# A two-block network on one core: an early table load, a planner that knows more of its transfers, and new offsets

## The chip, the core and the metric

The kernel runs on one core of a Trainium2 chip. Time is device time of one execution in microseconds (us); lower is better. TensorE (PE) multiplies, VectorE (DVE), ScalarE (ACT) and GpSimd (POOL) work element by element, and transfers are issued from the queues of SyncE (SP) and ScalarE.

## The reference, cut to what matters

Sequence 256, width 1024, float32. `first_block` runs two layers, `second_block` two more:

```python
for i in range(2):                       # first_block
    x = x + 0.5 * swiglu(rmsnorm(x), gate, up, down)      # "ffn1", hidden 2816
    proj = rmsnorm(x) @ w_in                              # "mix1"
    x = x + concat(delta_rule_heads(proj), hyena(proj)) @ w_out
    x = x + 0.5 * swiglu(rmsnorm(x), gate, up, down)      # "ffn2"
x = rmsnorm(x)
for l in range(2):                       # second_block
    proj = rmsnorm(x) @ w_in_2                            # "mix2"
    x = x + (gated sum of attention, retention, short conv) @ w_out_2
    x = x + (silu(conv(h @ w_g)) * (h @ w_u)) @ w_ffn_out # "ffn3"
```

The mix1 part is a chunked delta rule (convolutions, a triangular solve) beside a Hyena branch, a long convolution in frequency space whose filter spectrum comes from a small network with three sines.

## The kernel before

All weights are cut on the host into 604 chunks of 128 x 1024 floats, in the order of use, and streamed through four buffers (`ws`). For each chunk ScalarE rounds to a high part (`wh`, in `split`) and another engine subtracts to get the low part (`wl`); TensorE then runs three products for each block (high by high, high by low, low by high) to keep float32 accuracy. The first two chunks (`HEAD`) are moved and split in halves (`pieces`). The operation tags `pmm` and `pacc` are the two kinds of PSUM buffer; `c` stands for working tiles, `sm` for small ones, `x` for the residual.

A generator (`drive`) notes the whole program as some thousands of operations with their dependences; nothing is sent to an engine yet. `Plan.place` then lists them on a modelled clock: every engine takes, of the operations that are ready and have buffers, the one of highest rank. A rank is the modelled length of work that still depends on the operation, plus an offset from the table `AHEAD`, looked up by stage and part (`"ffn1 norm0"` is the first norm in its stage, `" x0"`, `" cst"` and `" "` are parts of `setup`). The stage's letters are the first four of its name. An operation in `either` goes to GpSimd at every n-th of its kind, n from the table `POOL`, else to VectorE. `nc.hold` is the earliest modelled time. `emit` writes each engine's list in the planned order, so the order on each in-order queue is what the plan decides; the plan's times themselves are not sent.

What the plan assumes of transfers stands in few lines:

```python
if ops[i].dma and bus > t + BACK:        # too much is under way: try later
...
hw = max(hw, t) + o.dma
now[e] = t + .06 if e != "POOL" else t + 1.1
bus = max(bus, hw + .8) + o.cost         # cost: bytes / 360e3 us
o.end = bus
```

`setup` issues x in four pieces of two feature tiles each (with the first gain) on ScalarE's queue, then the constants `cst` and the parameters `par`; `prep` makes high and low parts of x times gain and the squares, `norm` the token sums, their inverse root (`rsqrt_m`, eleven small VectorE operations) and `spread`, two transposes that turn it into the tile `r`. `spectra` (three sines, five results of each order written to DRAM as `ds`) runs as a side task, and `hyena` reads `ds` back; both use ScalarE's queue for it. The delta rule's `dn_solve` sends blocks through DRAM (`dg`, `dv`) on SyncE's queue.

Of the kernel before, what the change touches and what calls it, by code (L numbers as in the profile page):

```python
# [14 lines left out]
AF = mybir.ActivationFunctionType  # L15
# [9 lines left out]
EPS = 1e-6  # L25
CW = 1024
A3 = (2,)
BACK = 5
AHEAD = {' cst': -57, ' prep': 0, ' sq0': 25, ' x0': 82, 'conv': 5, 'cst': -50, 'da': 40, 'decay': 10, 'double': -20, 'ffn1 finish': 60, 'ffn1 norm': 110, 'ffn1 norm0': 5, 'ffn1 prep': 10, 'ffn1 sq': 25, 'ffn2 finish': -4, 'ffn2 prep': 40, 'ffn2 scaled': 0, 'ffn2 spec': 85, 'ffn2 split': 5, 'ffn3 finish': -40, 'ffn3 norm': 0, 'ffn3 prep': 40, 'ffn3 scaled': 42, 'ffn3 split': -7, 'ffn3 sq': 48, 'finish': 82, 'g0': 5, 'hyena': 10, 'kk': -10, 'mix1 double': 30, 'mix1 finish': 83, 'mix1 hyena': 20, 'mix1 kk': 10, 'mix1 out': 78, 'mix1 prep': 38, 'mix1 qk': 66, 'mix1 solve': 20, 'mix1 sq': 32, 'mix1 w': 3, 'mix2 finish': 12, 'mix2 norm': 162, 'mix2 prep': -40, 'mix2 ret': 95, 'mix2 split': -22, 'mix2 sq': 5, 'norm': 153, 'norm0': 152, 'out': 80, 'prep': 10, 'qk': 23, 'ret': 168, 'solve': 10, 'spec': 80, 'split': -2, 'sq': 28, 'sq0': 40, 'w': 8, 'x0': 2}
WIN = 1500  # L30
LOCK = True
RG = 2
SLACK = 2
HEAD = 2
NARROW = 5
PAD = 0.05
POOL = {'ba': 1, 'by': 1, 'gate': 4, 'hg': 3, 'ht': 2, 'hx0': 2, 'hx1': 4, 'hx3': 2, 'mask': 1, 'rot': 4, 'rvg': 1, 'sc': 2, 'sc1': 6, 'se': 4, 'v1': 6, 'wo2': 2}
GATES = [("gate", 0), ("gate", 1), ("gate", 2)] + [(k, m + 3 * (k == "gate")) for m in range(5) for k in ("br", "gate")] + [("br", m) for m in (5, 6, 7)]
WS, WP = 4, 4
HALF = (1, 0)  # L40
# [283 lines left out]
class Plan:  # L324
# [43 lines left out]
    @staticmethod  # L368
    def cost(eng, call, out, ins, kw):
        n = int(np.prod(out.shape[1:]))  # L370
        in_psum = any(a.tensor.space == PSUM for a in ins if type(a.tensor).__name__ == "Tile")
        if call == "dma_start":
            return out.shape[0] * n * 4 / 360e3 * (1.0 if n > 300 else 1.6)
        if eng == "PE":
            if call != "matmul":
                return .109
            n = int(np.prod(ins[-1].shape[1:]))
            if ins[-1].dtype == F32R:
                return .0049 + max(n, 256) * .0004426
            return 2 * (.005 + max(2 * n, 256) * .000418)  # L380
        n = max([n] + [int(np.prod(a.shape[1:])) for a in ins])
        ptr = sum(1 for a in ins[1:] if int(np.prod(a.shape[1:])) == 1 and n > 1)
        if eng == "DVE":
            if call == "memset":
                return .01 + n / 970
            one = call in ("tensor_scalar", "tensor_copy") and not in_psum
            return .068 + n * (.00052 if one else .00104) + .061 * ptr
        if eng == "ACT":
            return (.052 if in_psum else .094) + n * .000833 + .093 * (ptr + ("accum_out" in kw))
        if eng == "POOL":  # L390
            if call == "memset":
                return .035 + n / 1200
            return .15 + n * {"tensor_tensor": .0021, "affine_select": .00087}.get(call, .0031)
        raise AssertionError((eng, call))
# [46 lines left out]

    def lag(self, a, b):
        if a.dma:
            return .95
        return self.LAG.get((a.eng, b.eng), .25 if b.eng == "PE" else .13)

    def place(self):
        ops = self.ops
# [53 lines left out]
        pend = {e: [] for e in now}  # L502
        events = [0.0]
        back, far, lo = [], [], 0
        hw = bus = 0.0
        port = {"DVE": 0.0, "POOL": 0.0}
        table = None
        done = 0
# [5 lines left out]
        while done < len(ops):  # L514
# [10 lines left out]
            for e in now:  # L525
                while pend[e] and pend[e][0][0] <= t + 1e-9:
                    i = heapq.heappop(pend[e])[1]
                    heapq.heappush(wait[e], (-ops[i].rank, i))
                if now[e] > t + 1e-9:
                    continue  # L530
                skip, got = [], None
                while wait[e]:
                    r, i = heapq.heappop(wait[e])
                    if i > lo + WIN:
                        heapq.heappush(far, (i, r))
                        continue
                    if LOCK and ops[i].port and port[e] > t + 1e-9:
                        skip.append((r, i))
                        heapq.heappush(events, port[e])
                        continue  # L540
                    if ops[i].dma and bus > t + BACK:
                        skip.append((r, i))
                        heapq.heappush(events, bus - BACK)
                        continue
                    need = {}
                    for nm in ops[i].tiles:
                        if nm not in held:
                            need[self.tag[nm]] = need.get(self.tag[nm], 0) + 1
                    short = [g for g, n in need.items() if free[g] < n]
                    if short:  # L550
                        parked[short[0]].append((e, r, i))
                    elif i > lo and not safe(i):
                        unsafe.append((e, r, i))
                    else:
                        got = i
                        break
                for s in skip:
                    heapq.heappush(wait[e], s)
                if got is None:
                    continue  # L560
                o = ops[got]
                for nm in o.tiles:
                    if nm not in held:
                        held[nm] = True
                        free[self.tag[nm]] -= 1
                        live[self.tag[nm]][lo:span[nm][0]] += 1
                o.start = t
                if got == lo:
                    while lo < len(ops) and ops[lo].start is not None:
                        lo += 1  # L570
                    wake(unsafe)
                    heapq.heappush(events, t)
                while far and far[0][0] <= lo + WIN:
                    i, r = heapq.heappop(far)
                    heapq.heappush(wait[ops[i].eng], (r, i))
                    heapq.heappush(events, t)
                if o.dma:
                    hw = max(hw, t) + o.dma
                    now[e] = t + .06 if e != "POOL" else t + 1.1
                    bus = max(bus, hw + .8) + o.cost  # L580
                    o.end = bus
                else:
                    c = o.cost
                    if o.flex and e == "POOL":
                        c = o.flex
                    if o.table is not None and o.eng == "ACT":
                        s = "sin" if o.table == AF.Sin else "exp" if o.table in (AF.Exp, AF.Tanh) else table
                        if s != table:
                            c += 1.3
                            table = s  # L590
                    if e == "PE":
                        c += 1.7 * min(max(t - now[e] - 1.1, 0.0) / 2.2, 1.0)
                    now[e] = o.end = t + c
                    if o.port:
                        port["POOL" if e == "DVE" else "DVE"] = o.end
                heapq.heappush(events, now[e])
                done += 1
                for j in o.succs:
                    p = ops[j]
                    p.left -= 1  # L600
                    p.ready = max(p.ready, o.end + self.lag(o, p))
                    if not p.left:
                        heapq.heappush(pend[p.eng], (max(p.ready, t), j))
                        heapq.heappush(events, max(p.ready, t))
                for nm in o.tiles:
                    todo[nm] -= 1
                    last[nm] = max(last[nm], o.end)
                    if not todo[nm]:
                        live[self.tag[nm]][lo:span[nm][1] + 1] -= 1
                        x = last[nm] + (1.0 if o.dma else .2)  # L610
                        heapq.heappush(back, (x, self.tag[nm]))
                        heapq.heappush(events, x)
# [12 lines left out]
class Build:  # L625
# [316 lines left out]
    def setup(self):  # L942
# [13 lines left out]
            nc.scalar.dma_start(out=xg[:, c], in_=A["x"][:, c])  # L956
        nc.part = "cst"
        nc.scalar.dma_start(out=self.cst, in_=A["cf"])
        nc.part = ""
        nc.scalar.dma_start(out=self.par, in_=A["par"])  # L960
        nc.hold = 12.0
        self.rounded(self.cr.rearrange("p a b -> p (a b)"), A["cr"])
# [1148 lines left out]
```

## Time and profile before

| | us |
|---|---|
| median of 3 runs | 1942.88 |
| lowest and highest | 1941.55, 1950.27 |
| profiled execution, its own time | 1946.58 |
| span of the profiled execution | 1944.9 |

The span runs from the first to the last instruction of the program in the profiled execution; 1.7 us of that execution's time lie around it. All of the helpers' operations carry one line number, so the profile is read by tile names.

### The profile page before, as it was taken

Reading aid. Unit: us, or ns where it says so; the run is one execution under the profiler, and the core shown is the slowest. Engines: PE = TensorE matmul, PEld = TensorE weight load, DVE = VectorE, ACT = ScalarE, POOL = GpSimd, SP = SyncE. Lnnn points to the kernel's source line nnn. Section 1 sums busy time; section 2 is a strip of 40 time slices with the busy share of each in tenths; the row PEclk is TensorE's granted clock in tenths of the full one; section 3 lists DMA queues with packets and bytes.
Section 4 is the critical chain, followed back from the end, with each engine's and each line's share of the span. In section 5 each row is a group of like instructions: output and inputs, shape, how many; then the busy total and the mean of one; then the engine's idle time right before and its main releaser. Section 6 shows DMA issues by size and latency. Waiting matters only on the chain.

```text
span 1944.9 us, 36536 instructions
## 1 busy us (share of the span) xinstructions
PE 1910.2 (98%) x14038; PEld 1800.6 (93%) x14038; DVE 1509.2 (78%) x3067; ACT 1090.5 (56%) x1792; POOL 213.1 (11%) x218
## 2 busy tenths in 40 slices
PE   7999998999999999999999999999999999999999
PEld 7998997999999999998999999999999999999998
DVE  7768879986669667899886679766977788669776
ACT  5656664565556555664555565455655654556564
POOL 0000041000000000222000002233000012240000
PEclk9999998999999999999999999999999999999999
DMA  8655763255555556552565544555555544555553
GB/s 293 212 185 170 230 195 103 91 197 189 184 186 178 189 186 217 201 149 85 166 195 186 189 167 163 180 185 187 183 186 192 174 153 161 191 182 191 188 185 130
DMA packets 127046, 348.84 MB, mean 179 GB/s; under 512 B 24758, under 2 KB 39960, under 8 KB 126872
## 3 DMA queue, kind: packets, MB, share of 16 engines
q1 hardware_dynamic: 115584, 326.89, 51.3%
q10 hardware_dynamic: 11288, 19.63, 2.9%
q8 instruction: 110, 1.80, 0.4%
q14 instruction: 64, 0.52, 0.1%
HBM read 333.61 MB, written 11.81 MB: 178 GB/s over the span
## 4 chain that ended last, share of the span: by engine, by line
PE 91%; DVE 5%; ACT 1%; DMA 1%; issue 1%; ACTq 0%; POOL 0%; SPq 0%; DVEq 0%; POOLq 0%
PE pmm L621 57%; PE pacc L621 35%; DVE c L621 4%; DVE wl L621 1%; ACT c L621 1%; ACTq L621 0%; ACT wh L621 0%; DVE sm L621 0%; DVE x L621 0%; DMA ds<-c 0%; DMA c<-dv 0%; DMA ws<-in_W 0%; DMA x<-in_x 0%; POOL c L621 0%; ACT L621 0%
## 5 line engine op out<-in xcount | busy, mean ns | idle before, releaser
L621 PE MATMUL pmm<-c,wh 128*128 128x256 f32 (+1 forms) x4576 | 1102.4, 322 | 9.9 <-ACT wh L621 8.6
L621 ACT ACTIVATE wh<-ws 128x1024 fp32r<-128x1024 f32 (+1 forms) x604 | 635.6, 1055 | 537.0 <-PE pmm L621 221.3
L621 DVE TENSOR_TENSOR wl<-ws,wh 128x1024 fp32r<-128x1024 f32 (+1 forms) x562 | 687.7, 1226 | 270.9 <-ACT wh L621 265.0
L621 PE MATMUL pmm<-c,wl 128*128 128x256 f32 x3056 | 859.6, 281 | 0.1
L621 PEld LDWEIGHTS pmm<-c,wh 128*128 128x128 f32 x4576 | 759.8, 189 | 81.1 <-ACT wh L621 8.6
L621 PEld LDWEIGHTS pmm<-c,wl 128*128 128x128 f32 x3056 | 577.6, 189 | 1.0 <-DVE wl L621 0.6
L621 PE MATMUL pacc<-c,wh 128*128 128x256 f32 x3136 | 566.9, 281 | 0.0
L621 PEld LDWEIGHTS pacc<-c,wh 128*128 128x128 f32 x3136 | 482.6, 189 | 6.1 <-issue 0.7
L621 PE MATMUL pacc<-c,wl 128*128 128x256 f32 x1568 | 440.5, 281 | 0.0
L621 PEld LDWEIGHTS pacc<-c,wl 128*128 128x128 f32 x1568 | 296.0, 189 | 0.0
L621 ACT ACTIVATE c<-c 128x256 fp32r<-128x256 f32 (+4 forms) x412 | 181.2, 450 | 157.2 <-DVE c L621 144.3
L621 DVE TENSOR_TENSOR c<-c,c 128x256 f32<-128x256 f32 (+7 forms) x345 | 166.9, 497 | 7.9 <-ACT c L621 4.4
L621 DVE TENSOR_TENSOR c<-pmm,c 128x256 f32<-128x256 f32 (+1 forms) x292 | 134.5, 461 | 41.9 <-PE pmm L621 36.0
L621 DVE SCALAR_TENSOR_TENSOR c<-c,c 128x256 f32<-128x256 f32 (+3 forms) x288 | 129.3, 450 | 14.3 <-ACT c L621 7.7
L621 POOL TENSOR_TENSOR wl<-ws,wh 128x1024 fp32r<-128x1024 f32 x42 | 104.2, 2480 | 263.3 <-ACT wh L621 145.0
L621 DVE SCALAR_TENSOR_TENSOR c<-c,par,c 128x256 f32<-128x256 f32 x248 | 114.7, 482 | 22.9 <-ACT c L621 21.7
L621 PE MATMUL pacc<-c,c 128*128 128x128 f32 (+5 forms) x700 | 98.9, 302 | 2.8 <-DVE c L621 1.4
L621 ACT ACTIVATE c<-pacc 128x512 f32<-128x512 f32 (+4 forms) x125 | 59.2, 495 | 64.3 <-PE pacc L621 60.2
L621 POOL TENSOR_TENSOR c<-c,c 128x256 f32<-128x256 f32 (+1 forms) x50 | 60.9, 1222 | 291.6 <-DVE c L621 245.5
L621 PEld LDWEIGHTS pacc<-c,c 128*128 128x128 f32 (+2 forms) x700 | 83.1, 195 | 8.9 <-DVE c L621 2.3
L621 ACT ACTIVATE c<-c,par 128x256 f32<-128x256 f32 x96 | 52.8, 574 | 51.0 <-DVE c L621 50.4
L621 DVE TENSOR_TENSOR c<-pacc,c 128x512 f32<-128x512 f32 (+4 forms) x126 | 72.0, 610 | 9.3 <-PE pacc L621 6.6
(85 smaller groups left out, 997.6 us busy)
## 6 DMA issues: line engine op xcount, KB each, us to landing
ws<-in_W SPq DMA_DIRECT2D x600, 512.0 KB, 3.4
ds<-c ACTq DMA_DIRECT2D x20, 256.0 KB, 4.7
c<-ds ACTq DMA_DIRECT2D x20, 256.0 KB, 3.8
c<-dv SPq DMA_DIRECT2D x32, 128.0 KB, 2.7
dv<-c SPq DMA_DIRECT2D x8, 256.0 KB, 5.0
dg<-c SPq DMA_DIRECT2D x8, 256.0 KB, 3.2
c<-in_cm ACTq DMA_DIRECT2D x6, 256.0 KB, 5.0
ws<-in_W SPq DMA_DIRECT2D x4, 256.0 KB, 6.4
```

The costliest lines, as they stand in the source:

```text
L621: getattr(e, call)(*a, **kw)
```

## The change

ScalarE gets one Tanh of four zeros early in `setup`, on a tile that VectorE clears; nothing reads its result. The planner's transfers are costed at 330e3 bytes per us for 360e3; the bus is taken as busy up to 3.0 at the start; a transfer may not be planned while the eighth before it is unfinished (`lanes`); an issue takes .35 on ScalarE's queue for .06 (GpSimd's 1.1 goes too, but no transfer is issued there); a transfer on ScalarE's queue that depends on another is planned 6.5 behind its end for .95; the allowed backlog `BACK` is 3.0 for 5. The whole table `AHEAD` and the table `POOL` have new values.

```diff
-BACK = 5
-AHEAD = {' cst': -57, ' prep': 0, ' sq0': 25, ' x0': 82, 'conv': 5, ..., 'ffn1 norm0': 5, ..., 'hyena': 10, 'mix1 hyena': 20, 'mix1 qk': 66, 'mix1 solve': 20, 'norm': 153, ...}
+BACK = 3.0
+AHEAD = {' ': 65.0, ' cst': 43.0, ' prep': -38.0, ' sq0': 177.0, ' table': 111.0, ' x0': 68.0, 'conv': -109.0, ..., 'ffn1 norm0': 428.0, ..., 'hyena': -12.0, 'mix1 hyena': 32.0, 'mix1 qk': 400.0, 'mix1 solve': 83.0, 'norm': 302.0, ...}
-SLACK = 2
+SLACK = 2.0
-POOL = {'ba': 1, 'by': 1, 'gate': 4, 'hg': 3, 'ht': 2, 'hx0': 2, 'hx1': 4, 'hx3': 2, 'mask': 1, 'rot': 4, 'rvg': 1, 'sc': 2, 'sc1': 6, 'se': 4, 'v1': 6, 'wo2': 2}
+POOL = {'br': 3, 'hg': 6, 'ht': 2, 'hx0': 2, 'hx1': 3, 'mask': 1, 'rot': 4, 'rvg': 1, 'sc': 2, 'sc1': 3, 'se': 4, 'sh': 4, 'sq': 6, 'wo2': 4}
...
-            return out.shape[0] * n * 4 / 360e3 * (1.0 if n > 300 else 1.6)
+            return out.shape[0] * n * 4 / 330e3 * (1.0 if n > 300 else 1.6)
...
         if a.dma:
-            return .95
+            return 6.5 if b.dma and b.eng == "ACT" else .95
...
-        hw = bus = 0.0
+        hw, bus = 0.0, 3.0
+        lanes = [0.0] * 8
...
-                    if ops[i].dma and bus > t + BACK:
+                    if ops[i].dma and max(bus - BACK, lanes[-8]) > t:
                         skip.append((r, i))
-                        heapq.heappush(events, bus - BACK)
+                        heapq.heappush(events, max(bus - BACK, lanes[-8]))
...
-                    now[e] = t + .06 if e != "POOL" else t + 1.1
+                    now[e] = t + (.06 if e == "SP" else .35)
                     bus = max(bus, hw + .8) + o.cost
                     o.end = bus
+                    lanes.append(bus + .2)
...
         nc.scalar.dma_start(out=self.cst, in_=A["cf"])
-        nc.part = ""
+        nc.part, nc.hold = "table", .35
+        z = self.T("sm", [128, 2, 2])
+        nc.vector.memset(z[:, 0], 0.0)
+        self.act(z[:, 1], z[:, 0], AF.Tanh)
+        nc.part, nc.hold = "", 0.0
         nc.scalar.dma_start(out=self.par, in_=A["par"])
```

## Rows read from the trace of the kernel before

**Rows 1.** The page, busy time of each engine, its share of the span, instructions.

```profile
PE 1910.2 (98%) x14038; PEld 1800.6 (93%) x14038; DVE 1509.2 (78%) x3067; ACT 1090.5 (56%) x1792; POOL 213.1 (11%) x218
```

**Rows 2.** Waits of PE, whole span: us in total, times, longest us.

```profile
PE pacc L621 <- DVE c L621: 8.6, 13, 1.2
PE pmm L621 <- ACT wh L621: 8.6, 1, 8.6
...
PE pacc L621 <- DVE sm L621: 3.5, 2, 3.0
```

**Rows 3.** The chain that ended last, first 60 us: start us, us, what.

```profile
0.80 4.10 DMA x<-in_x
...
4.92 0.33 ACTq L621
...
5.28 1.28 ACT L621
...
6.58 1.43 ACT c L621 x3
...
13.93 4.38 DMA ws<-in_W
...
18.33 0.33 ACTq L621
...
18.70 0.44 ACTq L621
```

**Rows 4.** The groups by line, ACT's table loads: count, busy us, mean ns, idle before.

```profile
L621 ACT ACT_TABLE_LOAD x13 | 16.7, 1283 | 5.5 <-DMA x<-in_x 5.3
```

**Rows 5.** Timeline of DVE, 6 to 26 us: start us, us, what, idle before and its end.

```profile
16.75 0.15 DVE L621 TENSOR_SCALAR sm<-pacc 128x2 f32<-128x2 f32 x1
20.29 1.23 DVE L621 TENSOR_TENSOR wl<-ws,wh 128x1024 fp32r<-128x1024 f32 x1 [3.38 <-ACT wh L621]
```

**Rows 6.** Windows of the start: us, busy by engine (PE, PEld, DVE, ACT, POOL), PEclk, DMA, GB/s.

```profile
8.58:21.10 12.52, 12.42 (x76) 11.67 (x76) 9.11 (x17) 7.57 (x15) 0.00 (x0) 1.00 0.90 327
21.10:24.10 3.00, 0.00 (x1) 0.00 (x1) 2.69 (x14) 2.13 (x3) 0.00 (x0) 1.00 1.03 395
...
25.00:29.00 4.00, 4.00 (x24) 4.00 (x23) 3.38 (x10) 2.83 (x7) 1.01 (x1) 0.57 0.92 287
```

**Rows 7.** Timeline of ACT, 240 to 262 us, its queue and engine.

```profile
253.27 0.48 ACTq L621 DMA_DIRECT2D c<-in_hyf  x1
...
253.78 1.54 ACTq L621 DMA_DIRECT2D c<-in_cdec  x2
255.36 0.75 ACTq L621 DMA_DIRECT2D c<-in_hyf  x1
256.16 1.06 ACT L621 ACTIVATE wh<-ws 128x1024 fp32r<-128x1024 f32 x1 [2.26 <-PE pacc L621]
```

**Rows 8.** Windows around mix1 of either layer, and mix2: columns as Rows 6.

```profile
200.00:262.00 62.00, 59.16 (x427) 54.86 (x426) 48.36 (x118) 36.98 (x62) 13.71 (x17) 0.97 0.71 232
...
300.00:330.00 30.00, 22.68 (x133) 19.20 (x131) 26.60 (x60) 12.73 (x27) 6.69 (x7) 0.83 0.42 114
...
780.00:835.00 55.00, 54.05 (x431) 52.02 (x431) 47.93 (x126) 35.41 (x56) 8.90 (x14) 1.00 0.62 211
835.00:925.00 90.00, 83.68 (x650) 79.40 (x649) 87.18 (x224) 50.57 (x100) 20.27 (x20) 0.96 0.39 108
...
1270.00:1400.00 130.00, 130.00 (x1093) 129.74 (x1092) 93.81 (x153) 71.63 (x107) 35.08 (x30) 1.00 0.57 185
...
1350.00:1400.00 50.00, 50.00 (x418) 49.74 (x417) 46.66 (x93) 30.32 (x49) 0.92 (x7) 1.00 0.61 199
```

**Rows 9.** Groups by shape, DVE and POOL: count, busy us, mean ns, idle before.

```profile
L621 DVE TENSOR_TENSOR wl<-ws,wh 128x1024 fp32r<-128x1024 f32 x558 | 685.1, 1230 | 270.9 <-ACT wh L621 265.0 <-PE pmm L621 2.5
...
L621 DVE TENSOR_TENSOR c<-c,c 128x256 f32<-128x256 f32 x138 | 58.4, 423 | 3.2
...
L621 POOL TENSOR_TENSOR c<-c,c 128x256 f32<-128x256 f32 x32 | 34.2, 1075 | 59.7 <-DVE c L621 58.8
```

More of the change, by code (lines that the diff above doesn't have):

```diff
@@ L27 @@
 A3 = (2,)
-BACK = 5
-AHEAD = {' cst': -57, ' prep': 0, ' sq0': 25, ' x0': 82, 'conv': 5, 'cst': -50, 'da': 40, 'decay': 10, 'double': -20, 'ffn1 finish': 60, 'ffn1 norm': 110, 'ffn1 norm0': 5, 'ffn1 prep': 10, 'ffn1 sq': 25, 'ffn2 finish': -4, 'ffn2 prep': 40, 'ffn2 scaled': 0, 'ffn2 spec': 85, 'ffn2 split': 5, 'ffn3 finish': -40, 'ffn3 norm': 0, 'ffn3 prep': 40, 'ffn3 scaled': 42, 'ffn3 split': -7, 'ffn3 sq': 48, 'finish': 82, 'g0': 5, 'hyena': 10, 'kk': -10, 'mix1 double': 30, 'mix1 finish': 83, 'mix1 hyena': 20, 'mix1 kk': 10, 'mix1 out': 78, 'mix1 prep': 38, 'mix1 qk': 66, 'mix1 solve': 20, 'mix1 sq': 32, 'mix1 w': 3, 'mix2 finish': 12, 'mix2 norm': 162, 'mix2 prep': -40, 'mix2 ret': 95, 'mix2 split': -22, 'mix2 sq': 5, 'norm': 153, 'norm0': 152, 'out': 80, 'prep': 10, 'qk': 23, 'ret': 168, 'solve': 10, 'spec': 80, 'split': -2, 'sq': 28, 'sq0': 40, 'w': 8, 'x0': 2}
+BACK = 3.0
+AHEAD = {' ': 65.0, ' cst': 43.0, ' prep': -38.0, ' sq0': 177.0, ' table': 111.0, ' x0': 68.0, 'conv': -109.0, 'cst': -119.0, 'da': -84.0, 'decay': -170.0, 'double': 63.0, 'ffn1 finish': 51.0, 'ffn1 norm': 525.0, 'ffn1 norm0': 428.0, 'ffn1 prep': 22.0, 'ffn1 scaled': -1.0, 'ffn1 spec': 80.0, 'ffn1 split': -2.0, 'ffn1 sq': 210.0, 'ffn2 ': 5.0, 'ffn2 finish': 206.0, 'ffn2 norm': 257.0, 'ffn2 prep': 477.0, 'ffn2 scaled': -39.0, 'ffn2 spec': 71.0, 'ffn2 split': 92.0, 'ffn2 sq': 211.0, 'ffn3 ': 0.0, 'ffn3 finish': -79.0, 'ffn3 norm': 51.0, 'ffn3 prep': 126.0, 'ffn3 scaled': 129.0, 'ffn3 split': -69.0, 'ffn3 sq': -140.0, 'finish': 188.0, 'hyena': -12.0, 'kk': 139.0, 'mix1 ': -1.0, 'mix1 conv': 5.0, 'mix1 decay': 10.0, 'mix1 double': 267.0, 'mix1 finish': -134.0, 'mix1 hyena': 32.0, 'mix1 kk': 10.0, 'mix1 norm': 249.0, 'mix1 out': 87.0, 'mix1 prep': 81.0, 'mix1 qk': 400.0, 'mix1 solve': 83.0, 'mix1 split': -2.0, 'mix1 sq': 13.0, 'mix1 w': 3.0, 'mix2 da': 40.0, 'mix2 finish': 10.0, 'mix2 norm': 157.0, 'mix2 prep': -127.0, 'mix2 ret': 167.0, 'mix2 split': -157.0, 'mix2 sq': -113.0, 'norm': 302.0, 'norm0': -78.0, 'out': 72.0, 'prep': -329.0, 'qk': 234.0, 'ret': 123.0, 'scaled': -344.0, 'solve': 55.0, 'spec': -6.0, 'split': -74.0, 'sq': -34.0, 'sq0': -38.0, 'table': 17.0, 'w': 20.0, 'x0': 190.0}
 WIN = 1500
```

## The prediction

> **What bounds the kernel now.** I read the busy times first, then PE's waits, then the chain and the windows of the stretches in which PE stood. PE is busy 1910.2 of 1944.9 us [rows 1], and the change takes no product away, so what it can give back is PE's idle time, 34.7 us, and what a lower TensorE clock costs just after an idle stretch. Of the waits, one of 8.6 us is the start, before the first product, and one of 3.0 us comes a little later, on a small DVE tile; the waits on DVE's working tiles are 13, 8.6 us together [rows 2]. The windows show where these lie: around mix1 of both layers, with DVE near its limit. PE is full in the window of mix2 that I took [rows 8].
>
> **The start, step by step.** The chain shows the first piece of x in flight from 0.80 for 4.10 us, an issue on ACT's queue at 4.92, the table load of 1.28 us at 5.28, three operations on x, and only then the first split of weights [rows 3]. The 13 loads of the run are one here and two around each of six sines, at 1283 ns each [rows 4], so one load serves all functions but the sine. The Tanh takes the load ahead of x's landing if it stands in ACT's queue before the issue that waits at 4.92 (it starts 0.02 us after x landed: a transfer waits for an earlier one to finish, which is what the new limit of eight models). In the new plan the backlog limit of 3.0 holds up further issues as soon as the first pieces are under way, ACT then has nothing else ready, and the Tanh goes in behind the first piece of x. I take the whole 1.3 us. Below, the gain is nothing if the waiting issue still stands ahead, and the price is up to 1.6 us if the other three pieces of x, now issued behind memset, load and Tanh, become what is late (the load's 1.28 and about 0.3 for the two small operations, an estimate from the small DVE row of 0.15 [rows 5]). What would hide the load is the 4.10 us of x.
>
> Here the Trainium skill has another price: "ScalarE: Activation LUTs", section "What ACT_TABLE_LOAD costs", adds a drain of about 1380 ns to a load's 1283. The trace shows the 1283 but no drain: the next operation starts at 6.58, 1.30 behind the load's start [rows 3]. By the page the head would give 2.7 us and the sum below would be 1.4 lower.
>
> Next the norm. DVE does its first small operation at 16.75, then stands 3.38 us in front of a split at 20.29 whose high part is not made [rows 5], with the rest of the inverse root behind it; PE stands from 21.10 to 24.10, and at 25 to 29 its granted clock is 0.57 of full, most of that time at the lower level, which costs 0.43 x 4.00 = 1.7 us [rows 6]. The high part was late because ACT's queue stood: its issue at 18.33 starts 0.02 us behind the landing of a weight chunk (13.93 + 4.38), then one more issue of 0.44 [rows 3]. Both causes are addressed: the offset of this norm goes from 5 to 428, far ahead of the splits, and the limit of eight puts blocking issues elsewhere. Without the split in front, the inverse root ends before PE needs it. So 3.0 + 1.7 are open, with the load 6.0. But the chunk split at 20.29 is ready at 21.5 and PE, 1.3 us ahead, would want it at 19.8: 1.7 us late next, if its landing does not move. I give back 1.5: **-4.5** for the start. Bounds: -6.0 and +1.6.
>
> Against more speak the transfers: their engines are busy 0.90 and 1.03 of the time from 8.58 to 24.10 [rows 6]. If that is the limit the chunk cannot land earlier, and the start gives only the 2.6 us from 21.5 to 24.1. The Trainium skill, "DMA: Bandwidth & Descriptors", section "Issuing engines are not separate DMA queues", says why it may be: transfers of all queues share the same engines and interleave, so another order of issue moves bytes, it does not add any.
>
> **Layer 0 before mix1's end.** From 200 to 262, PE is idle 2.84 us and the clock of 0.97 costs some 1.8 [rows 8]. Four issues fill ACT's queue from 253.27 to 256.11, 0.69 us each, and a split waits behind them [rows 7]; the old plan gave them 0.06, the new one 0.35. What is late after them is that split's chunk. I take the longest of the waits here, near 1.1, and half of the clock: **-2.0**. Bounds 0 and -4.6. The 6.5 behind a dependent transfer acts on the same queue, for `ds`; it is in this term.
>
> **The ends of mix1.** From 300 to 330, PE is idle 7.32 us, and the clock of 0.83 costs 0.17 x 22.68 = 3.9; from 835 to 925, 6.32 and 0.04 x 83.68 = 3.3 [rows 8]. Together 20.8, the largest sum that the offsets can reach. But DVE is busy 26.60 of 30 and 87.18 of 90 there: the stall ends only if DVE work is done before or behind these stretches. There is room before: 13.6 us free from 200 to 262, 7.1 from 780 to 835. Chains bind, though: the delta rule cannot start before its projections. And the new POOL table gives DVE splits in mix1: the two of `ba`, two of `hx3`, one of `v1`, less one of `hx1`, net four at 1.23 [rows 9], 4.9 us, where DVE is the limit. Between +4.9 and -14 (two thirds), I take a third: **-7.0**, nearer to the full DVE than to its free room ahead.
>
> **Other edits.** In mix2 each layer's DVE gets six `gate` splits (7.4), sixteen `by` additions at 0.42 (6.8) and two `wo2` splits (2.5) and gives three `br` splits (3.7): 13.0 net [rows 9]. DVE's free time hides them, 36.2 of 130 us [rows 8]; without that cover they cost what the third rival says. The bandwidth of 330 and the bus at 3.0 move only orders and are in the start. A new order makes new waits: I add three at the mean of 0.66 us (8.6 over 13) [rows 2], **+2.0**; below nothing is not to be had from this.
>
> **Sum.** -4.5 - 2.0 - 7.0 + 2.0 = -11.5. The profiled execution took 1946.58, span 1944.9 and 1.7 around it: 1935.1. It stands 3.7 above the median of the three runs, 1942.88, so the median should come to 1931.4.
>
> **Rivals.**
> First: the ends of mix1 stay, because DVE has no room that its chains can use. Speaking for it, 87.18 of 90; against it, the free room ahead. Then -4.5 - 2.0 + 2.0: 1938.4; with the 4.9 us of returned splits, 1943.3.
> Second: the load does not get ahead, being queued behind the issue that waits for x. For it, the two waits of 0.02 us behind a landing; against it, the backlog limit. The forecast loses 1.3: 1932.7. It may go with any case and decides none. The full transfer engines at the start are of this kind too: 4.5 becomes 2.6, 1933.3.
> Third, on the other side: DVE becomes the bound at mix2's end. In the last 50 us of that stage DVE is busy 46.66, 3.3 free [rows 8]; POOL's additions take 1075 ns and DVE's 423 [rows 9], but POOL's ran beside it. Once more than 3.3 of the 13.0 us fall into that stretch, PE waits; with all of them it is 9.7 a layer, 19.4 for both. On the first rival's time this is 1957.8. Against it: most gates come earlier, where DVE has its room.
> Fourth: all of the start, 6.0, all of layer 0's lead, 4.6, and two thirds of the ends, 14, less the 2.0: 1942.88 - 22.6 = 1920.3.
>
> **How the numbers follow.** Forecast 0.55, with 1925 to 1937 as its own range; first rival 0.22; third 0.10; fourth 0.10; 0.03 for some slower mishap without a name. 0.5% is 9.7 us, about what the runs can tell from no change: faster means under 1933.2, slower over 1952.6. The forecast's own range puts two thirds below that line, 0.37; with the fourth, faster 0.47. The rest of the forecast, 0.18, and the first rival make 0.40 for the same; slower 0.13. From 1919 to 1946 the range leaves out the third rival and the nameless one, 0.13, and about half of the fourth.
>
> **What would show it.** The load starting near 1.3 to 3 us and the first product near 7.3; no wait of PE of 3 us on a small DVE tile; the clock not falling near 25; ACT's queue without a row of issues in front of a split near 253; PE's idle time around mix1's ends down from 13.6 to some 9. The forecast is wrong if DVE in those windows is as full and PE as idle as now, or if new PE waits on `wl` stand at the end of mix2.

## The result, and the profile after

The changed kernel takes 1925.03 us, the median of four runs (1923.67 to 1925.60); the kernel before, in the same comparison, 1945.37 (1941.55 to 1950.27). The ratio is 0.9893, with an interval of 0.9867 to 0.9919: 1.1% faster, clear of the scatter. Beside the experiments the kernel before has medians of 1942.87, 1944.94 and 1943.91, so the gain is 18 to 21 us. The profiled execution's span is 1923.8 us for 1944.9, 21.1 less. The execution profiled before took 1946.58, 1.2 to 3.7 us above the medians of its kernel, so not all of the 21.1 is the change's.

The page of the changed kernel, the first line busy time by engine (us, share of the span, instructions); then PE's waits (us in total, times, longest us):

```profile
PE 1900.1 (99%) x14038; PEld 1794.1 (93%) x14038; DVE 1533.7 (80%) x3106; ACT 1087.9 (57%) x1791; POOL 157.0 (8%) x180
```

```profile
PE pmm L623 <- ACT wh L623: 7.4, 2, 6.6
PE pacc L623 <- DVE c L623: 5.3, 8, 2.4
PE pacc L623 <- ACT c L623: 2.7, 4, 1.4
PE pmm L623 <- DVE wl L623: 2.2, 2, 1.1
PE pacc L623 <- POOL c L623: 1.5, 1, 1.5
```

PE's idle time is 1923.8 - 1900.1 = 23.7 us, for 34.7 [rows 1]. The wait of 3.0 us on a small DVE tile [rows 2] is gone, and the waits on DVE's working tiles are 8 with 5.3 us, for 13 with 8.6. DVE gained 24.5 us of work and lies at 80%, POOL lost 56: work went from the engine that had time to the much fuller one, and PE stands less all the same. A fuller DVE did not cost PE time here.

To see where the 21.1 us came from, both spans are cut where the same amount of PE's work is done (after product 500, 2000, 5500 and 9500 of the 12336 products of a working tile `c` with a weight's `wh` or `wl`; the PE counts of the pairs agree within two). First the kernel before, then the changed one; columns as in [rows 6].

```profile
0.00:83.70 83.70, 72.02 (x508) 68.12 (x509) 62.60 (x120) 48.54 (x79) 3.91 (x12) 0.98 0.78 262
83.70:386.60 302.90, 292.64 (x2075) 270.47 (x2073) 247.83 (x572) 173.50 (x293) 43.45 (x47) 0.98 0.51 163
386.60:955.90 569.30, 561.75 (x4076) 527.28 (x4075) 450.20 (x913) 318.64 (x528) 38.87 (x45) 0.99 0.55 178
955.90:1533.70 577.80, 576.83 (x4283) 546.69 (x4282) 436.91 (x835) 323.48 (x527) 65.16 (x64) 1.00 0.55 182
1533.70:1944.90 411.20, 406.92 (x3106) 387.99 (x3104) 311.71 (x630) 226.36 (x368) 61.69 (x50) 1.00 0.52 172
```

```profile
0.00:79.60 79.60, 71.09 (x507) 67.61 (x508) 60.73 (x113) 45.99 (x77) 5.32 (x13) 0.98 0.81 276
79.60:375.30 295.70, 289.82 (x2077) 268.42 (x2075) 250.28 (x580) 173.44 (x293) 38.63 (x44) 0.99 0.51 169
375.30:937.70 562.40, 557.53 (x4076) 525.18 (x4075) 450.00 (x913) 318.30 (x529) 39.72 (x47) 0.99 0.54 179
937.70:1512.00 574.30, 574.00 (x4282) 544.07 (x4281) 448.04 (x854) 323.48 (x527) 37.93 (x45) 1.00 0.54 183
1512.00:1923.80 411.80, 407.63 (x3106) 388.83 (x3104) 324.63 (x649) 226.66 (x368) 35.46 (x31) 1.00 0.51 172
```

| stretch, by work | length | of it, PE's idle time |
|---|---|---|
| the start | -4.1 | -3.2 |
| to the end of layer 0's mix1 | -7.2 | -4.4 |
| to the end of layer 1's mix1 | -6.9 | -2.7 |
| layer 0 of the second block and beyond | -3.5 | -0.7 |
| the rest | +0.6 | -0.1 |
| together | -21.1 | -11.0 |

(Length is the difference of the first numbers of two lines; idle time is the first less the second number.) So the gain lies where the prediction looked, the start and both mix1 parts, but 3.5 us come from a stretch where none was expected, and nearly half of the whole is not idle time.

The start of the changed kernel, ACT's timeline (start us, us, queue or engine, what, how many, idle before and its end):

```profile
0.80 0.42 ACTq L623 DMA_DIRECT2D x<-in_x  x1
1.25 1.28 ACT L623 ACT_TABLE_LOAD   x1 [1.25 <-PEq L2106]
1.31 1.35 ACTq L623 DMA_DIRECT2D x<-in_x  x3
2.54 0.20 ACT L623 ACTIVATE sm<-sm 128x2 f32<-128x2 f32 x1
4.99 1.03 ACT L623 ACTIVATE c<-x 128x512 f32<-128x512 f32 x2 [2.24 <-DMA x<-in_x]
...
10.79 0.33 ACTq L623 DMA_DIRECT2D cst<-in_cf  x1
```

The load runs at 1.25, beside the three other issues of x, and the first operation on x starts at 4.99 for 6.58 [rows 3]. The issue of `cst`, which stood at 4.92 just behind x's landing [rows 3], is now at 10.79. What PE meets then:

```profile
6.59 0.80 PE L623 MATMUL pmm<-c,wh 128*128 128x256 f32 x2 [6.59 <-ACT wh L623]
...
13.21 0.50 PE L623 MATMUL pmm<-c,wh 128*128 128x256 f32 x2 [0.84 <-ACT wh L623]
```

The first product comes 2.0 us sooner than the 8.6 of [rows 2], but 0.84 us is lost again at 12.37, where the next chunk's high part is late.

The windows of the changed kernel that answer to [rows 6, 8]:

```profile
12.37:14.79 2.42, 0.50 (x3) 0.30 (x2) 2.10 (x4) 2.42 (x5) 0.50 (x1) 1.00 0.71 224
15.00:19.00 4.00, 4.00 (x22) 4.00 (x22) 3.01 (x6) 0.95 (x1) 0.00 (x0) 0.57 0.86 286
200.00:262.00 62.00, 62.00 (x480) 59.19 (x480) 55.54 (x140) 39.27 (x65) 12.59 (x14) 1.00 0.67 231
290.00:330.00 40.00, 34.16 (x237) 30.54 (x236) 36.45 (x85) 20.02 (x41) 10.18 (x11) 0.91 0.33 91
780.00:835.00 55.00, 55.00 (x450) 53.78 (x449) 49.66 (x134) 36.79 (x66) 16.47 (x19) 1.00 0.71 227
835.00:925.00 90.00, 85.13 (x645) 80.23 (x644) 88.09 (x258) 45.46 (x81) 12.65 (x13) 0.96 0.36 112
```

The lead of layer 0's mix1 (200 to 262) has no idle time left and a full clock. Of the 1.9 us that PE stands from 12.37 to 14.79, 0.84 and 1.08 are waits for a weight's high and low part; the granted clock then falls (0.57 from 15 to 19, as it was from 25 to 29). At the ends of mix1 PE still stands 5.84 and 4.87 us, for 7.32 and 6.32, and DVE is as full as before.

How much of the clock is the change's? In the run e17 (below) TensorE's 14038 products stand in the very order of the kernel before. Here is one window of the kernel before, then two of e17:

```profile
220.00:223.00 3.00, 3.00 (x16) 3.00 (x15) 3.00 (x13) 0.63 (x1) 0.00 (x0) 0.50 0.52 177
```

```profile
200.00:262.00 62.00, 60.38 (x451) 56.31 (x450) 49.79 (x123) 37.95 (x63) 15.48 (x17) 1.00 0.70 231
220.00:223.00 3.00, 3.00 (x24) 2.87 (x24) 3.00 (x11) 1.73 (x3) 0.00 (x0) 1.00 0.22 76
```

In the kernel before the clock stood at its lower level from 220 to 223, although TensorE had not been idle since 200. Ten small products in a row come just before it (217.24 to 219.5). In e17 the same ten run from 216.32 to 218.6, and the clock stayed full. So a fall need not follow an idle stretch, and one order of products can have it in one execution and not in another. An estimate from windows of 4 us (busy time times what the clock lacks to 1.00): the lower clock cost PE 10.8 us in the trace before and 5.0 in e17, 6.7 in the changed kernel and 5.2 in e16, which has the changed kernel's order. The clock's share of a difference between two traces is thus not shown to be the change's.

### The profile page after: what moved, and what is told of

The parts are those of the page before. It is cut to its first block, busy times and chain, and to the rows that moved or that the text cites. A ratio compares the mean times of both kernels' runs of the same rounds, so it can differ in the third digit from the quotient of the medians.

```text
span 1923.8 us, 36454 instructions
## 1 busy us (share of the span) xinstructions
PE 1900.1 (99%) x14038; PEld 1794.1 (93%) x14038; DVE 1533.7 (80%) x3106; ACT 1087.9 (57%) x1791; POOL 157.0 (8%) x180
## 4 chain that ended last, share of the span: by engine, by line
PE 93%; DVE 5%; issue 1%; ACT 0%; DMA 0%; POOL 0%; ACTq 0%; DVEq 0%
PE pmm L623 58%; PE pacc L623 35%; DVE c L623 3%; DVE wl L623 1%; DMA x<-in_x 0%; DVE sm L623 0%; ACT c L623 0%; DVE x L623 0%; POOL c L623 0%; ACTq L623 0%; ACT wh L623 0%; ACT L623 0%; DVEq L623 0%; ACT sm L623 0%
## 5 line engine op out<-in xcount | busy, mean ns | idle before, releaser
L623 DVE TENSOR_TENSOR wl<-ws,wh 128x1024 fp32r<-128x1024 f32 (+1 forms) x576 | 702.5, 1223 | 254.8 <-ACT wh L623 249.1
L623 DVE TENSOR_TENSOR c<-c,c 128x256 f32<-128x256 f32 (+8 forms) x369 | 173.0, 480 | 8.1 <-ACT c L623 4.6
L623 DVE SCALAR_TENSOR_TENSOR c<-c,par,c 128x256 f32<-128x256 f32 x248 | 115.5, 483 | 21.3 <-ACT c L623 21.0
L623 POOL TENSOR_TENSOR wl<-ws,wh 128x1024 fp32r<-128x1024 f32 x28 | 69.6, 2487 | 299.2 <-ACT wh L623 200.7
L623 POOL TENSOR_TENSOR c<-c,c 128x512 f32<-128x512 f32 (+1 forms) x26 | 34.8, 1340 | 551.5 <-DVE c L623 249.0
```

The source lines that it names most:

```text
L623: getattr(e, call)(*a, **kw)
```

## The experiments

Two accounts were to be told apart. One: the early load and a cleaner start bring the gain, the rest is small. The other: the order as a whole brings it, either by the new tables alone, by the planner's new figures alone, or only by tables made for a planner that is nearer to the chip. Each time below is a median, beside a median of the kernel before on the same chip; the ratio is taken over all their runs and need not be the quotient of the two medians. "Figures" are the planner's new figures for transfers, "tables" are `AHEAD` and `POOL`.

| run | what is new in it | us | before | ratio (interval) |
|---|---|---|---|---|
| e1_table_only | Tanh | 1941.48 | 1942.87 | 0.9988 (0.9979 to 0.9998) |
| e3_model_only | planner's figures | 1942.99 | 1942.87 | 0.9996 (0.9987 to 1.0004) |
| e5_offsets_only | tables | 1948.82 | 1942.87 | 1.0023 (1.0012 to 1.0033) |
| e2_no_table | figures, tables | 1930.53 | 1942.87 | 0.9928 (0.9916 to 0.9940) |
| e6_old_offsets | Tanh, figures | 1940.48 | 1944.94 | 0.9975 (0.9967 to 0.9984) |
| e7_old_pool | all but `POOL` | 1933.00 | 1944.94 | 0.9941 (0.9927 to 0.9954) |
| e8_no_lag | all but the 6.5 | 1940.17 | 1944.94 | 0.9980 (0.9971 to 0.9989) |
| e16_same_order_no_load | all, Tanh not sent | 1924.35 | 1944.94 | 0.9895 (0.9882 to 0.9909) |
| e17_cst_behind | one issue moved | 1942.50 | 1943.91 | 0.9995 (0.9986 to 1.0003) |
| s1_old_searched | other tables | 1936.13 | 1943.91 | 0.9964 (0.9951 to 0.9977) |
| s2_new_from_old | Tanh, figures, other tables | 1928.24 | 1943.91 | 0.9922 (0.9909 to 0.9935) |
| s3_new_searched | Tanh, figures, other tables | 1925.55 | 1943.91 | 0.9906 (0.9893 to 0.9919) |

**The Tanh alone**, in the kernel before:

```diff
+        nc.part, nc.hold = "table", .35
+        z = self.T("sm", [128, 2, 2])
+        nc.vector.memset(z[:, 0], 0.0)
+        self.act(z[:, 1], z[:, 0], AF.Tanh)
+        nc.part, nc.hold = "", 0.0
```

> The kernel before with the early Tanh alone, planner and tables as before. If the load in front of x's use is a loss of its own: first product near 7.3 for 8.58, time 1 to 2 us under the kernel before. If the start is held by the transfers that follow: first product earlier, time the same within 1 us. The 3 us wait of PE near 21 us stays by either.

It took 1941.48. The first product comes at 7.08, 1.5 us sooner, and the run gains 1.4. PE's wait on the small DVE tile stays, 2.53 us. The early load is a small part of the 18 to 21.

**The change without the Tanh:**

```diff
-        nc.part, nc.hold = "table", .35
-        z = self.T("sm", [128, 2, 2])
-        nc.vector.memset(z[:, 0], 0.0)
-        self.act(z[:, 1], z[:, 0], AF.Tanh)
-        nc.part, nc.hold = "", 0.0
+        nc.part = ""
```

> The changed kernel without the Tanh. If the load is worth its length: 1.3 to 2 us over the changed kernel's 1925.0. If the whole gain hangs on ScalarE's early queue: 4 us or more over it, since the order planned around the load shifts too.

It took 1930.53, 5.5 more than the changed kernel, as the second case had it. ACT's timeline of this run, and below it the first row of PE's:

```profile
4.89 0.33 ACTq L623 DMA_DIRECT2D cst<-in_cf  x1
6.84 0.53 ACTq L623 DMA_DIRECT2D c<-in_hyf  x1
7.41 1.28 ACT L623 ACT_TABLE_LOAD   x1 [7.41 <-DMA ws<-in_W]
8.70 2.47 ACT L623 ACTIVATE c<-x 128x512 f32<-128x512 f32 x5
```

```profile
14.27 1.02 PE L623 MATMUL pacc<-cst,c 128*128 128x1 f32 x4 [14.27 <-DVE c L623]
```

Not the load's 1.28 but the order cost this: two issues stand ahead of the load, five operations on x behind it, and the first weight's split behind those. By the plan (the kernel's program works it out, no measurement) the Tanh and its load fill ScalarE from 0.5 to 1.9 us and hold back three issues of x, so that the issue of `cst` comes at 9.9, behind eleven operations. Without the Tanh it comes at 3.2, ahead of all of them. So two things were still one here, the load's own place and the room that the planned Tanh takes.

**The same order, no Tanh.** The Tanh is planned as in the changed kernel but not sent; no output depends on it:

```diff
+            if ops[i].part == "table":
+                continue
```

> The changed kernel's own order with the Tanh planned but not sent, so that the load falls to ScalarE's first use. If the Tanh's direct worth is the load's length in front of x: 1.3 to 2 us over the changed kernel, 1926.3 to 1927. If it hides more than its length: the 5.5 us of the kernel without the Tanh, 1930.5; then the other 4 us there would not be the plan's.

It took 1924.35, the same as the changed kernel and under both times that were expected. ACT's timeline:

```profile
0.81 1.86 ACTq L625 DMA_DIRECT2D x<-in_x  x4
2.69 1.28 ACT L625 ACT_TABLE_LOAD   x1 [2.69 <-issue]
4.95 1.03 ACT L625 ACTIVATE c<-x 128x512 f32<-128x512 f32 x2 [0.97 <-DMA x<-in_x]
...
10.76 0.33 ACTq L625 DMA_DIRECT2D cst<-in_cf  x1
```

Nobody asks for the load early, and it still runs at 2.69, as soon as the queue is past the issues of x, and ends a microsecond before x lands. The load never waited for x. It waited for its turn behind the issue of `cst`. In this order the Tanh that is sent is worth nothing; the Tanh in the plan is worth some 5.5 us.

**That issue alone**, moved in the kernel before to behind the first three operations on x and the first split, no Tanh:

```diff
-        for i in sorted(range(len(ops)), key=lambda i: (ops[i].start, i)):
+        for i in sorted(range(len(ops)), key=lambda i: (ops[i].start + (2.4 if ops[i].dma and ops[i].part == "cst" else 0.0), i)):
```

> The kernel before with one move in ScalarE's queue: the issue of the constants goes behind the first three operations on x and the first split; no Tanh, planner and tables as before. If that issue, which waits for x, is what held the table load: load near 2.7, first product near 7.3, 1 to 1.5 us under the kernel before, as with the Tanh alone. If the load waits for x by itself: load at 5.3 and no gain.

ACT's timeline, and two rows of PE's:

```profile
0.80 1.86 ACTq L621 DMA_DIRECT2D x<-in_x  x4
2.69 1.28 ACT L621 ACT_TABLE_LOAD   x1 [2.69 <-issue]
4.93 1.43 ACT L621 ACTIVATE c<-x 128x512 f32<-128x512 f32 x3 [0.96 <-DMA x<-in_x]
...
6.54 0.33 ACTq L621 DMA_DIRECT2D cst<-in_cf  x1
```

```profile
6.93 0.79 PE L621 MATMUL pmm<-c,wh 128*128 128x256 f32 x2 [6.93 <-ACT wh L621]
...
23.23 0.69 PE L621 MATMUL pacc<-cst,sm 128*128 128x128 f32 x2 [2.80 <-DVE sm L621]
```

One moved issue puts the load at 2.69 in the kernel before as well, and the first product at 6.93. That settles the mechanism of the load. Of the 1.65 us, 0.85 are left at product 500, the wait on the small tile stays at 2.80, and the whole time, 1942.50, can't be told from no change.

**The planner's figures alone**, with the old tables and no Tanh, and then with the Tanh (the diff is the second's, against the changed kernel; the first is the kernel before with the figures):

```diff
-AHEAD = {' ': 65.0, ' cst': 43.0, ' prep': -38.0, ...}
-POOL = {'br': 3, 'hg': 6, 'ht': 2, ...}
+AHEAD = {' cst': -57, ' prep': 0, ' sq0': 25, ...}
+POOL = {'ba': 1, 'by': 1, 'gate': 4, ...}
```

> The kernel before with the planner's new transfer figures alone; offsets, the GpSimd table as before, no Tanh. Theory 1 (the gain is the plan that knows its transfers): most of the 20 us, 1926 to 1932, no wait of 3 us near 21. Theory 2 (the gain is the new offsets): within 5 us of the kernel before. Theory 3 (each needs the other): a third or less of the gain, 1938 or more.

> Tanh and new planner, the old offsets and the old GpSimd table. If the late start of the model alone (first product at 14.2) came from planning without the Tanh: first product near 7 and about 5 us under the model alone, 1937 to 1938, and the rest to the changed kernel, 12 us, is the new tables'. If the old offsets are as good under a planner that is right: 1930 or less.

Without the Tanh 1942.99, nothing; PE's first wait is 13.4 us there, the same late start as in the run without the Tanh above. With it 1940.48, 4.5 under its own kernel before. The two differences between with and without the Tanh, 5.5 and some 4.6, are alike: under the new figures a plan without the Tanh starts late.

With it the start is already the changed kernel's. PE's only waits from 8 to 60 us are these, with that of 3.0 us on a small tile gone:

```profile
PE pmm L623 <- ACT wh L623: 1.0, 1, 1.0
PE pmm L623 <- DVE wl L623: 1.0, 1, 1.0
```

By 50 us PE has worked 41.00 us, for 41.49 in the changed kernel and 38.32 before. So the start's gain comes from the figures and the Tanh and needs no new offsets. The time is above the 1937 to 1938 expected, and the tables bring 16 us more, not 12 (1940.48 to the 1924.35 measured beside it).

**The tables alone**, with the old planner: the two lines above the other way round, in the kernel before.

> The kernel before with the new offsets and the new GpSimd table alone; the planner's old transfer figures, no Tanh. Theory 1: little, 1938 or more, ScalarE's queue still blocked behind transfers. Theory 2: most of the gain, 1926 to 1932. Theory 3: a third or less, or even slower than before, since the offsets were made for another planner.

1948.82, 5.9 slower. ACT's timeline shows one place; 2.2 us are lost up to product 500:

```profile
14.41 1.56 ACT L621 ACTIVATE wh<-ws 128x512 fp32r<-128x512 f32 x2
...
20.31 0.44 ACTq L621 DMA_DIRECT2D c<-in_hyf  x1
23.38 0.37 ACTq L621 DMA_DIRECT2D c<-in_oh  x1
...
24.27 0.21 ACT L621 ACTIVATE sm<-par 128x8 f32<-128x8 f32 x1 [8.30 <-DMA c<-in_hyf]
```

The old planner gives an issue 0.06 us and lets small transfers go one after the other; on the chip they wait their turn. ACT computes nothing for 8.3 us, and its splits stand behind them.

**The old `POOL` table, and the old lag**, each in the changed kernel:

```diff
-POOL = {'br': 3, 'hg': 6, 'ht': 2, 'hx0': 2, ...}
+POOL = {'ba': 1, 'by': 1, 'gate': 4, 'hg': 3, ...}
```

> The changed kernel with the old GpSimd table. If the shares of GpSimd matter little: within 2 us of the changed kernel. If fewer splits on GpSimd are part of the gain, or the offsets fit only their own shares: 4 us or more over it, lost at the ends of mix1.

```diff
-            return 6.5 if b.dma and b.eng == "ACT" else .95
+            return .95
```

> The changed kernel with .95 for 6.5 behind a transfer that ScalarE's queue depends on. If this delay is what frees ScalarE's queue: ScalarE blocked behind ds again, PE waits near mix1, 5 to 12 us over the changed kernel. If the start and the backlog are what matter: within 3 us.

With the old `POOL` table 1933.00, 8.6 over the 1924.35 measured beside it. The windows of this run around layer 0's mix1, in an execution of 1937.38, the slowest of its five:

```profile
200.00:262.00 62.00, 61.23 (x434) 56.79 (x433) 49.50 (x123) 38.56 (x64) 15.43 (x17) 0.94 0.63 215
290.00:330.00 40.00, 32.96 (x210) 28.65 (x209) 37.60 (x94) 19.92 (x39) 6.89 (x7) 0.85 0.38 107
```

Both lose what the change had won there: PE's idle time is 0.77 and 7.04 us for 0 and 5.84, the clock 0.94 and 0.85 for 1.00 and 0.91. How much of the clock is this execution's own is open.

With the old lag 1940.17, 15.8 over, more than the 5 to 12 expected, and not because ScalarE stands behind `ds` again. Its stretches of over 0.3 us with neither work nor issue that end at an issue (without that of the result at the end) come to 4.9 us here, to 4.2 in the changed kernel and to 12.6 in the kernel before. What grew are PE's waits on DVE's working tiles, 8 with 5.3 us in the changed kernel and here:

```profile
PE pacc L623 <- DVE c L623: 13.3, 10, 5.3
```

The longest lasts from 865 to 870, near the end of layer 1's mix1. What the lag changed there is open. These two runs say what a part is worth beside tables made for the whole, not what it would be worth with tables of its own.

**Tables of its own for each planner.** Offsets were changed at random, steps kept that shorten the planner's own length: for the old planner from the old tables, for the new one (with the Tanh) from the old tables and from the new.

```diff
-AHEAD = {' cst': -57, ' prep': 0, ' sq0': 25, ...}
-POOL = {'ba': 1, 'by': 1, 'gate': 4, ...}
+AHEAD = {' ': 73.0, ' cst': 208.1, ' prep': -0.8, ...}
+POOL = {'ba': 5, 'br': 4, 'by': 3, ...}
```

(the diff of the first; the other two have tables of their own in the same two lines)

> The kernel before with other offsets and GpSimd shares, found by random steps on the old planner's own length: 1910.3 by its clock, for 1917.9 of the kernel before and 1913.5 of the changed one by the new clock. If what the planner believes of transfers decides: its error stays near 25 us, 1933 to 1938. If a searched table is what brings the gain, whichever planner: 1920 to 1925.

> Tanh and new planner, with tables found by random steps that start at the old tables: 1913.5 by the planner's clock, as the changed kernel. If the planner's length tells the time: 1924 to 1929. If the changed kernel's own tables hold something that length does not see: 1933 or more.

> The changed kernel with tables found by random steps that start at its own: 1911.3 by the planner's clock, 2.2 less. If that length still tells the time: 1922 to 1924. If what is left is below what the planner can tell: 1925 to 1930.

1936.13, 1928.24 and 1925.55, beside 1943.91 before. So new tables by themselves, found for the old planner, bring 7.8 us; the planner's figures and the Tanh another 7.9 to 10.6. Each is the outcome of one random search, and how far another search would have come was not tried. No version is clearly faster than the changed kernel.

The planner's own length of each order (worked out by the kernel's program, no measurement) points to why. Against the measured medians:

```
old planner   planned  measured     new planner   planned  measured
before        1917.9   1942.9       after         1913.5   1925.0
Tanh alone    1918.0   1941.5       no Tanh       1915.1   1930.5
tables alone  1923.8   1948.8       figures alone 1926.2   1943.0
searched      1910.3   1936.1       from old      1913.5   1928.2
```

The old planner falls short by 23.5 to 25.8 us, the new one by 11.5 to 16.8. Within the old one, differences come true: the tables alone are 5.9 longer by plan and 5.9 on the chip, the searched ones 7.6 shorter by plan and 7.8 beside their own kernel before. What it can't see is a part of some 25 us that every order carries, and no table made under it shortens what it doesn't see. The new figures put 8.3 us of that into the plan for the old tables: the planned length rises to 1926.2, the chip's time stays, and new tables then bring both down. Within the new planner small differences do not come true: the orders "after" and "from old" have one planned length and measure 3.2 us apart, and the one planned at 1911.3 (s3) measured 1925.55.

Is the part now seen the waits of issues on ACT's queue? By the sum used above for the old lag, these are 12.6 to 21.3 us before, with the tables alone and with the searched ones, and 2.8 to 7.7 in the traces with the new figures. So they do go. But the run with Tanh, figures and old tables has only 4.1 of them and still takes 1940.48. That they are what the tables then shorten was not shown.

## Why the prediction was right, point by point

The time lies in the range, the case was the forecast's, and the sign is right. But 1925.03 is 6.4 us under the 1931.4 of the sum and at the very edge of the forecast's own 1925 to 1937. The gain was foreseen as 11.5 us and measured as 18 to 21, in spans 21.1. By the steps:

- **The start, -4.5: measured -4.1, by another road.** The load did go ahead of x and is hidden by x's flight, as forecast, and the issues of x were not held up. Full transfer engines did not cap it at 2.6 either: they moved the same 22 MB in 79.6 us for 83.7. But "the Tanh takes the load ahead if it stands in ACT's queue before the issue that waits" names the needed thing and gives it to the wrong part: it is the moved issue of `cst` that frees the load, Tanh or no Tanh. The second rival's premise (the load held by the issue that waits) was the kernel before exactly. The page of the Trainium skill weighed there, "ScalarE: Activation LUTs", section "What ACT_TABLE_LOAD costs", adds a drain of about 1380 ns to a load. Here the load starts at 1.25 and lasts 1.28, and an operation starts at 2.54, so again no drain shows.
- **The norm.** The 3.0 us of PE [rows 6] went, as did the fall of the clock at 25. In their place came 0.84 and 1.08 us for a chunk and a fall of the clock at 15: the step "1.7 us late next" was right in kind and near in size, at an earlier chunk, and the clock's price was not saved, only moved. That the offset of 428 did it is not so: put alone into the kernel before, it leaves the order on every engine as it was, so it could change no time. The limit of eight did not do it either, since without it the changed kernel's order is the same on every engine (both by the kernel's program). The run with Tanh, figures and old tables lost the wait too. Which of the figures did it was not tried on the chip.
- **Layer 0's lead, -2.0: measured -4.6, its bound, in part by luck.** Idle time 2.84 to 0, and 62 us at a clock of 1.00 for 0.97 [rows 8]. The step had the split's chunk late behind the row of issues. What PE waited for there, 1.14 us at 258.73, was a working tile of ScalarE made behind that split; its other two waits, 1.21 and 0.49, lie ahead of those issues. No issue stands in ScalarE's queue from 245 to 262 any more. The 1.8 us of clock need not be the change's: e17, with the old order, has 1.00 there too.
- **The ends of mix1, -7.0: about -3.8.** Idle time fell by 1.5 and 1.5, the clock's price in layer 0 from 3.9 to 0.09 x 34.16 = 3.1. The idle time around both ends together is 10.7 us, for 13.6 before and the 9 given as a sign. The first rival had the mechanism: DVE is as full as before (88.09 of 90). The windows of layer 0 do not quite cover the same work, so this is good to a microsecond.
- **New waits, +2.0: wrong as a charge on top.** Three did come, of 0.84, 1.08 and 1.09 us, on a weight's high and low parts, and they are inside the figures above. On DVE's working tiles there are 8 waits, not 16, and in mix2 only one of 0.2, though DVE got its additional work there: free time hid it, and the third rival fell. Instead of a loss the stretch through layer 0 of the second block gained 3.5.
- **What the sum had no term for.** Of the 21.1 us, 11.0 are idle time. The busy time of PE fell by 10.1 for the same 14038 products. The clock makes some 4 of it (10.8 for 6.7), as much as executions of one order differ by. Without the clock's part the busy time is 1899.4 before and 1901.0 in e17, 1893.3 in the changed kernel and 1893.1 in e16: 6 us or more go with the order, 2.8 of them in the fourth stretch, where the clock is 1.00 in both. What shortens it is open; no run was made for it.

So the places were right. Of the causes, the waiting issue and the full DVE were right, the offset and the limit of eight were not. The lead was sized too small, the ends of mix1 too large, the charge for new waits was wrong, and the terms as measured make 12.5 of the 21.1 us. That the errors of lead and ends nearly cancel is luck. Adding up idle stretches one by one also left out what the runs show of the whole: figures alone gave 0.1 slower, tables alone 5.9 slower, the Tanh alone 1.4 faster, Tanh and figures 4.5 faster, and all of it 18 to 21 faster. The parts do not add: the tables fit the figures under which they were made.

## What to carry to other kernels

When one engine both computes and issues transfers, look in its queue for issues that stand behind a landing: what they delay is whatever is next on that engine, a table load included, and the remedy is the place of the issue. When an order is made by a planner, first compare its length with the chip's and mend what it leaves out, then make the offsets anew: the figures alone gave nothing, with the Tanh 4.5 us, tables found under the old figures 7.8, all together 18 to 21. And undo one part at a time only together with its tables, or the run says how well the old tables fit, not what the part is worth.

## What the runs showed that was not expected

- A load of a table does not wait for the data of the operation that needs it: it ran at 2.69, and the operation, which waited for x, at 4.95.
- A load runs beside issues on the same engine: three issues from 1.31 to 2.66 beside the load from 1.25 to 2.53.
- One order can meet the lower clock at other places from one execution to the next: the kernel before and e17 have the same 14038 products in the same order, and from 220 to 223 the clock was 0.50 in one and 1.00 in the other. A fall of the clock in one trace is no proof of what the order costs.
- The scatter of times goes with the clock. Of the kernel before, 21 runs beside the second group of experiments lie between 1941.1 and 1951.3; its runs at a mean granted clock of 0.995 to 0.997 take 1941.1 to 1943.9, those at 0.991 to 0.994 take 1943.9 to 1951.3. In the other groups the two overlap (1945.8 at 0.995). The changed order, with the Tanh sent or not, has eight runs at 0.995 to 0.997, all within 2 us.
